# The second mixer's triangular inverse: diagonal blocks packed in DRAM, four partitions for each, and a transpose on TensorE

## The chip, the cores and the metric

The kernel runs as one program on 1 core of one Trainium2 chip. The metric is the device time of that core in microseconds (us), the median over repeated runs. TensorE (PE in the rows; PEld is its weight load) does the matmuls, VectorE is DVE, ScalarE is ACT, GpSimd is POOL, and SyncE is SP, which here only issues DMAs. A line such as L403 is line 403 of the kernel before; lines of the changed kernel are named as such.

## The reference, cut to what matters

Two transformer blocks of width 1024 run over one sequence of 256 tokens. The second block's token mixer holds two linear recurrences, each with 4 heads of width 128: a gated delta rule (the kernel's `gdn`) and HGRN2 (the kernel's `hgrn`). Their gated outputs are joined and projected (`w_out`), and a mixture of 64 experts follows. The gated delta rule needs a unit lower triangular system solved per head and chunk:

```python
    L = jnp.where(strict, jnp.einsum('bhncd,bhnsd->bhncs', kb, kc) * decay, 0.0)
    rhs = jnp.concatenate([vc * bc[..., None], kb * jnp.exp(gc)[..., None]], axis=-1)
    sol = lax.linalg.triangular_solve(L + jnp.eye(CHUNK, dtype=L.dtype), rhs,
                                      left_side=True, lower=True, unit_diagonal=True)
...
    oB = hgrn2_chunked(qB, kB, iB.reshape(B, T, HG_HEADS, HG_DV), logf).reshape(B, T, HG_V)
    oB = rms_norm_2(oB, hg_norm_w) * jax.nn.silu(gateB)
    o = jnp.concatenate([oA, oB], axis=-1).astype(h.dtype)
    return jnp.einsum('bte,ed->btd', o, w_out)
```

The kernel works on chunks of 128 tokens, which the algebra allows: 8 systems (4 heads, 2 chunks) of 128x128.

## The kernel before, in words

**Weights.** Projection weights come from DRAM in units of 128x1024 fp32 (512 KB). SP's one queue loads a unit into `raw` (L274); ACT rounds it to `whi` (L324), and DVE, or POOL for a list of units, subtracts to get the remainder `wlo` (L325). Each product is then three matmuls per 128x128 weight tile: `whi` with the high part, `whi` with the low part, `wlo` with the high part (L330 to L332 in `linear`, L352, L357 and L358 in `pair`).

**The second mixer.** `second_block` keeps six generators: `k` is `proj_gdn`, `f` is `proj_hgrn`, `q` is `proj_qv`, `h` is `hgrn`, `d` is `gdn`, `g` is `proj_gates2`. A string of letters, `MIXER`, says in which order they are stepped, and so in which order the work is recorded; a scheduler then fixes one order of instructions for each engine when the program is built, from its own estimates of durations. On the chip each engine runs its list in that order and waits where an operand is missing. `proj_gates2` makes the output gates from four pairs of 128x256 products, 48 matmuls a pair (L1304 to L1315); these, and the short convolutions of the projections (L1145, three taps per tile on DVE), are the work that stands beside the inverse.

**The inverse.** `proj_gdn` ends with `inverse(L, 8, self.N, "ax")` (L1239). L holds 8 matrices of 128x128, tokens on partitions. Each is cut into a 4x4 grid of 32x32 blocks. `inverse` writes L to DRAM (`dl`, L421) and reads the 32 diagonal blocks back with one block per partition (`inst`, L424). `base_inverse` then inverts all 32 at once by a forward elimination of 31 steps, two DVE instructions a step (the product at L403 into `kt`, the subtraction at L404), each over 32 partitions and (31-j)(j+1) elements. ACT writes the transposes (L405), both forms go to DRAM (`da`, L435), and seven reads put them where the products want them: four into N (L439), three into Mc (L442). Then TensorE fills the blocks off the diagonal by products of 32x32 and 64x64 blocks (L413, copies between at L454 to L477). The last write of N is the copy at L477.

**After it.** `gdn` for two chunks of 128 tokens uses N; the copy of its last product from PSUM is at L1373. `hgrn` takes its two chunks one after the other; each goes through seven levels (differences L1435 and L1436 and a product L1438 on DVE, exp on ACT at L306, a product on POOL at L1439, four matmuls L1441, a masked copy L1447 on DVE) and a diagonal (L1445, and L1447 with the mask `masks`). The state between chunks is copied at L1467, the output at L1476. `gated` (L1388, L1389) multiplies by the gates, and `mix_half` runs the output projection (L1404). The first mixer of the kernel calls `inverse` too, with 16 systems and an `extra` argument (L724).

## Time and profile before

| | |
|---|---|
| median of 3 runs | 1160.67 us (1160.2 to 1164.21) |
| profiled execution | 1161.43 us, its span 1159.6 us |
| busy in the span | PE 1078.0 us (93%), DVE 678.1 (58%), ACT 437.1 (38%), POOL 240.3 (21%) |
| mean granted TensorE clock | 0.975 of full speed |

The span is the stretch between the first and the last recorded instruction; the profiled execution's own time is 1.83 us more. The share of busy time is a mean over stages with different limits: the recursion of the second inverse, its products and both recurrences of the mixer lie between about 600 and 705 us of the span, and what limits that stretch is read there.

### The profile page before, as it was taken

The numbers are of one execution on the slowest core, as the hardware profiler recorded it, in microseconds if no ns is written. First come the engines' busy times: TensorE is split into PE (matmuls) and PEld (weight loads), VectorE is DVE, ScalarE is ACT, GpSimd is POOL, SyncE is SP. The second block draws the span as 40 slices with busy tenths as digits, with TensorE's granted clock in tenths as the row PEclk, the third lists the DMA queues.
The fourth block names the chain that finished last, engine by engine and source line by source line (L and its number), as shares of the span: only waits on it lengthen the run. The fifth ranks groups of instructions, "written<-read, shape, count | busy, mean of one in ns | idle before, by whom it ended". The sixth has DMA issues, their size and how long they took to land.

```text
span 1159.6 us, 20386 instructions
## 1 busy us (share of the span) xinstructions
PE 1078.0 (93%) x8050; PEld 824.7 (71%) x8050; DVE 678.1 (58%) x1211; ACT 437.1 (38%) x707; POOL 240.3 (21%) x245
## 2 busy tenths in 40 slices
PE   4989899999999999988979999999999999999995
PEld 4889787788989999987968889874444455444441
DVE  5598633356687888878799988432333333333333
ACT  5744433365454444335855645311111111111112
POOL 1251102023322001486461131320000000000000
PEclk9899979999999999999999999899999999999998
DMA  4445521025578998864434503969999999999993
GB/s 172 146 138 183 167 72 38 1 76 175 171 243 287 326 332 323 285 243 151 148 117 142 179 31 135 420 230 385 419 406 416 419 419 420 388 420 419 419 419 146
DMA packets 67496, 290.70 MB, mean 251 GB/s; under 512 B 15984, under 2 KB 17136, under 8 KB 46912
## 3 DMA queue, kind: packets, MB, share of 16 engines
q1 hardware_dynamic: 66528, 287.93, 66.3%
q8 instruction: 66, 1.08, 0.4%
q10 hardware_dynamic: 864, 1.38, 0.4%
q14 instruction: 38, 0.31, 0.1%
HBM read 285.77 MB, written 3.51 MB: 249 GB/s over the span
## 4 chain that ended last, share of the span: by engine, by line
PE 47%; DMA 17%; DVE 8%; ACT 4%; issue 4%; POOL 3%; SPq 0%; POOLq 0%; DVEq 0%; ACTq 0%
DMA er<-in_E_dram 12%; PE bank L1896 8%; PE p_b L357 4%; PE p_b L358 4%; PE p_b L352 4%; PE bank L1924 4%; PE acc L1793 3%; PE bank L1856 3%; DMA xa<-in_E_dram 3%; PE p_b L797 2%; POOL wlo L325 2%; ACT k L306 2%; PE p_b L332 2%; PE p_b L331 2%; PE p_b L330 2%
## 5 line engine op out<-in xcount | busy, mean ns | idle before, releaser
L324 ACT ACTIVATE whi<-raw 128x1024 fp32r<-128x1024 f32 x168 | 175.4, 1056 | 101.1 <-PE p_b L331 35.3
L325 DVE TENSOR_TENSOR wlo<-raw,whi 128x1024 fp32r<-128x1024 f32 x138 | 179.8, 1310 | 52.3 <-ACT whi L324 47.9
L358 PE MATMUL p_b<-k,wlo 128*128 128x256 f32 x608 | 173.6, 286 | 4.3 <-DVE wlo L325 2.4
L357 PE MATMUL p_b<-k,whi 128*128 128x256 f32 x608 | 173.9, 286 | 2.3 <-DVE k L325 2.3
L352 PE MATMUL p_b<-k,whi 128*128 128x256 f32 x608 | 173.5, 286 | 1.5 <-ACT whi L324 0.7
L332 PE MATMUL p_b<-k,wlo 128*128 128x256 f32 (+2 forms) x496 | 143.3, 294 | 14.5 <-DVE wlo L325 12.7
L330 PE MATMUL p_b<-k,whi 128*128 128x256 f32 (+2 forms) x496 | 145.5, 297 | 7.5 <-ACT k L324 4.1
L331 PE MATMUL p_b<-k,whi 128*128 128x256 f32 (+2 forms) x432 | 125.8, 294 | 2.1 <-DVE k L1126 1.1
L358 PEld LDWEIGHTS p_b<-k,wlo 128*128 128x128 f32 x608 | 116.6, 192 | 7.2 <-DVE wlo L325 3.0
L325 POOL TENSOR_TENSOR wlo<-raw,whi 128x1024 fp32r<-128x1024 f32 x30 | 81.0, 2704 | 193.8 <-ACT whi L324 193.1
L357 PEld LDWEIGHTS p_b<-k,whi 128*128 128x128 f32 x608 | 116.4, 192 | 3.7 <-DVE k L325 2.7
L352 PEld LDWEIGHTS p_b<-k,whi 128*128 128x128 f32 x608 | 116.3, 192 | 3.1 <-issue 0.9
L332 PEld LDWEIGHTS p_b<-k,wlo 128*128 128x128 f32 (+1 forms) x496 | 95.8, 195 | 17.3 <-DVE wlo L325 14.8
L330 PEld LDWEIGHTS p_b<-k,whi 128*128 128x128 f32 (+1 forms) x496 | 95.8, 195 | 13.3 <-ACT k L324 5.1
L1896 PE MATMUL bank<-er,x 128*32 128x512 f32 (+2 forms) x464 | 90.2, 595 | 3.3 <-DMA er<-in_E_dram 3.2
L1924 PE MATMUL bank<-er,k 128*32 128x512 f32 (+2 forms) x488 | 89.4, 595 | 2.6 <-DMA er<-in_E_dram 1.4
L1896 PE MATMUL bank<-er,h 128*32 128x512 f32 (+2 forms) x488 | 87.5, 595 | 0.0
L331 PEld LDWEIGHTS p_b<-k,whi 128*128 128x128 f32 (+1 forms) x432 | 84.5, 196 | 2.9 <-DVE k L1126 1.3
L1098 DVE SCALAR_TENSOR_TENSOR wada<-wada,crow 128x1024 f32<-128x1024 f32 x48 | 70.8, 1476 | 25.6 <-DMA wada<-in_W_ada_dram 25.3
L1844 POOL TENSOR_TENSOR k<-k,masks 128x128 f32<-128x128 f32 (+3 forms) x44 | 17.5, 430 | 316.0 <-DVE y L325 309.6
L1901 ACT ACTIVATE k<-bank 128x256 f32<-128x256 f32 x24 | 9.2, 385 | 194.6 <-PE bank L1896 194.6
L1902 DVE SCALAR_TENSOR_TENSOR k<-k,gs,bank 128x256 f32<-128x256 f32 x24 | 11.5, 480 | 100.1 <-ACT k L1901 100.1
(478 smaller groups left out, 2037.0 us busy)
## 6 DMA issues: line engine op xcount, KB each, us to landing
er<-in_E_dram SPq DMA_DIRECT2D x132, 1024.0 KB, 17.9
raw<-in_W_dram SPq DMA_DIRECT2D x168, 512.0 KB, 4.1
wada<-in_W_ada_dram SPq DMA_DIRECT2D x48, 512.0 KB, 5.7
xa<-in_E_dram SPq DMA_DIRECT2D x24, 1024.0 KB, 12.6
xa<-in_Sh_dram SPq DMA_DIRECT2D x2, 1024.0 KB, 8.3
k<-in_xT_dram SPq DMA_DIRECT2D x4, 272.0 KB, 5.0
dl<-x SPq DMA_DIRECT2D x1, 1024.0 KB
x<-in_xT_dram SPq DMA_DIRECT2D x1, 1024.0 KB
```

Of the source, the lines that this page charges most:

```text
L324: ins = self.nc.scalar.activation(hi, src, AF.Copy)
L325: (engine or self.nc.vector).tensor_tensor(lo, src, hi.bitcast(F32), op=OP.subtract)
L330: mm(out, w[0], x[0], start=start, stop=False)
L331: mm(out, w[0], x[1], start=False, stop=False)
L332: mm(out, w[1], x[0], start=False, stop=stop)
L352: a = mm(p[:, i], w[0], v[0], start=(n == 0), stop=False, **kw)
L357: mm(p[:, i], w[0], v[1], start=False, stop=False, **kw)
L358: mm(p[:, i], w[1], v[0], start=False, stop=last, **kw)
L1098: nc.vector.scalar_tensor_tensor(w, w, 1.0, c, op0=OP.mult, op1=OP.mult, accum_out=self.mod[:, o:o + 1])
L1793: self.nc.tensor.matmul(self.acc[t], w, x, start=t not in self.started, stop=False, skip_group_check=True)
L1896: mm(ph[t], X[:, k, i * 128 + t.start:i * 128 + t.stop], u[:, kk * 512:kk * 512 + 512], start=(k == 0), stop=(k == KD - 1), skip_group_che ...
L1924: nc.tensor.matmul(py[t], q.H[:, k, t], u[:, k * 1024 + c * 512:k * 1024 + c * 512 + 512], start=(k == 0), stop=(k == 1), skip_group_check ...
```

## The change

The inverse without `extra` (the second mixer's) goes through a new `by_columns`; with `extra` (the first mixer's) it goes through `by_blocks`, which holds the lines that were there. In `by_columns` the diagonal blocks alone are written to DRAM, one after the other (four writes of 32-KB pieces, 128 KB in all), and that 128 KB is read four times as a whole, to partitions 0 to 31, 32 to 63, 64 to 95 and 96 to 127. So every block stands on four partitions, and partition group c solves for columns c, c+4, c+8 and so on: 31 steps of two instructions as before, over 128 partitions and (31-j)(j//4+1) elements. ACT writes the transposes (128x256 elements), one write takes them to DRAM, and four reads put them into N. The blocks for Mc, which were read from DRAM, come from 8 transposes of N on TensorE (L389 by way of `tr`) and 6 copies on ACT (L444 of the changed kernel).

```diff
+    def by_columns(self, L, N, Mc, work, tag):
...
+        inst, M, MT = b(work[:, 1], 32), b(work[:, 2, :256], 8), b(work[:, 3, :256], 32)
+        u, flat = work[:, 2, 256:512], work[:, 2, :256]
+        nc.gpsimd.memset(flat, 0.0)
+        for c in range(4):
+            nc.gpsimd.memset(flat[32 * c:32 * c + 32, 8 * c::33], 1.0)
+        dl = self.dram.tile([4 * ns, 32, 32], F32, name=f"dl{ns}")
+        for k in range(4):
+            q = slice(32 * k, 32 * k + 32)
+            nc.sync.dma_start(dl[ns * k:ns * k + ns].rearrange("s t c -> t s c"), L[q, :, q])
+        for c in range(4):
+            nc.sync.dma_start(inst[32 * c:32 * c + 32], dl)
+        for j in range(31):
+            r, c = 31 - j, j // 4 + 1
+            v = u[:, :r * c].rearrange("p (a b) -> p a b", b=c)
+            nc.vector.tensor_tensor(v, inst[:, j + 1:, j:j + 1].to_broadcast([128, r, c]), M[:, j:j + 1, :c].to_broadcast([128, r, c]), op=OP.mult)
+            nc.vector.tensor_tensor(M[:, j + 1:, :c], M[:, j + 1:, :c], v, op=OP.subtract)
+        nc.scalar.activation(MT, M.rearrange("p a b -> p b a"), AF.Copy)
+        da = self.dram.tile([8, 128, 32], F32, name=f"da{ns}")
+        nc.sync.dma_start(da.rearrange("i p t -> p i t"), MT)
+        back = da.rearrange("i (c k s) t -> (i c) k s t", c=4, k=4)
+        for k in range(4):
+            q = slice(32 * k, 32 * k + 32)
+            nc.sync.dma_start(N[q, :, q], back[:, k])
+        yield
+        for h in (0, 4):
+            pt = b(self.psum(tag), 128)
+            for s in range(4):
+                self.tr(pt[:, s], N[:, h + s])
+            for k in range(3):
+                q = slice(32 * k, 32 * k + 32)
+                o = 32 * (k % 2)
+                nc.scalar.activation(Mc[q, h:h + 4, o:o + 32], pt[q, :, q], AF.Copy)
...
+        if not extra:
+            yield from self.by_columns(L, N, Mc, work, tag)
+        else:
+            yield from self.by_blocks(L, ns, N, Mc, work, extra)
```

The scheduler places the work after the recursion elsewhere. On TensorE, at the first product of the inverse, the order of before reads as follows; `p_b_7307` is the PSUM tile of the fourth and last pair of `proj_gates2`, and `p_b_6592` that of the inverse's first product.

```order
L357 MATMUL p_b_7307<-k_5673,whi 128x256
L358 MATMUL p_b_7307<-k_5672,wlo 128x256
L413 MATMUL p_b_6592<-k_6437,k_6075 32x32 x8
L352 MATMUL p_b_7307<-k_5672,whi 128x256
L357 MATMUL p_b_7307<-k_5673,whi 128x256
L358 MATMUL p_b_7307<-k_5672,wlo 128x256
```

In the order of the changed kernel (L413 is L481 there) the inverse's first product stands in the second pair, `p_b_7138`, and the transposes that feed Mc follow.

```order
L358 MATMUL p_b_7138<-k_5672,wlo 128x256
L352 MATMUL p_b_7138<-k_5672,whi 128x256
L481 MATMUL p_b_6609<-k_6437,k_6075 32x32 x8
L357 MATMUL p_b_7138<-k_5673,whi 128x256
L358 MATMUL p_b_7138<-k_5672,wlo 128x256
L1485 MATMUL p_b_7233<-h_7234 128x128 x4
L389 MATMUL p_b_6593<-masks,k_6437 128x128 x4
L389 MATMUL p_b_6601<-masks,k_6437 128x128 x4
L1485 MATMUL p_b_7245<-h_7246 128x128 x3
```

Before, 30 of the 48 matmuls of the fourth pair stand ahead of the inverse's first product; now 46 of 48 of the second pair do, and 83 matmuls of the third and fourth pairs come behind the inverse's last product, 79 of them ahead of `gdn`'s last (L1416 of the changed kernel).

On DVE, around `gdn`'s last copy, the order of before has the copy (L1373) among the levels of `hgrn`'s second chunk, whose tiles are the `h` from 7422 up; rows of the last four levels stand around it.

```order
L1447 COPY_PREDICATED h_7422<-offT,p_b_7454 128x512
L1435 TENSOR_TENSOR h_7503<-h_7424 128x128x2
L1436 TENSOR_TENSOR h_7503<-h_7424 128x128x2
L1438 TENSOR_TENSOR h_7503<-h_7503,h_7426 128x128x2
L1373 COPY k_6931<-p_b_7206 128x4x128
L1447 COPY_PREDICATED h_7422<-offT,p_b_7466 128x512
L1435 TENSOR_TENSOR h_7515<-h_7424 128x256
L1447 COPY_PREDICATED h_7422<-offT,p_b_7490 128x512
```

In the changed kernel that copy is L1417, the levels are L1479, L1480, L1482 and L1491, and the second chunk's tiles are the `h` from 7439 up.

```order
L1417 COPY k_6948<-p_b_7223 128x4x128
L1491 COPY_PREDICATED h_7060<-offT,p_b_7391 128x512
L1500 TENSOR_TENSOR h_7416<-h_7062 128x512
L1358 SCALAR_TENSOR_TENSOR k_6990<-p_b_7324,cols,ge 128x256 x2
L1502 TENSOR_TENSOR h_7416<-h_7416,h_7064 128x512
L1491 COPY_PREDICATED h_7060<-masks,p_b_7403 128x512
L1511 COPY h_7059<-p_b_7427 128x512
L1520 COPY k_7058<-p_b_7433 128x4x128
L1479 TENSOR_TENSOR h_7448<-h_7441 128x4x64
L1480 TENSOR_TENSOR h_7448<-h_7441 128x4x64
L1479 TENSOR_TENSOR h_7460<-h_7441 128x8x32
```

Before, `gdn`'s last copy comes after 18 of the second chunk's 21 differences and products; now the first chunk's last level, its diagonal and its state and output copies (`h_7058`, `h_7059`, `h_7060` and L1520) come behind `gdn`'s last copy, and the second chunk's first instruction is the ninth row.

## Rows read from the trace of the kernel before

**Rows 1.** Windows: stretch, length, busy us of PE, PEld, DVE, ACT, POOL; clock, DMA.

```profile
600.00:660.00 60.00, 50.01 (x396) 48.48 (x397) 58.62 (x118) 33.73 (x44) 12.97 (x7) 0.97 0.40 130
660.00:700.00 40.00, 37.78 (x353) 33.09 (x352) 32.82 (x58) 18.71 (x32) 13.08 (x14) 1.00 0.20 63
```

**Rows 2.** PE's timeline, 605 to 650: start, duration, instruction, wait and releaser.

```profile
607.33 0.39 PE L332 MATMUL p_b<-k,wlo 128*128 128x256 f32 x1 [4.71 <-DVE wlo L325]
...
649.17 0.39 PE L358 MATMUL p_b<-k,wlo 128*128 128x256 f32 x1 [1.61 <-DVE wlo L325]
```

**Rows 3.** DVE's timeline, the recursion of the second inverse from its first to last instruction.

```profile
600.53 0.72 DVE L403 TENSOR_TENSOR kt<-gate 32x31 f32<-32x31 f32 x1
601.28 0.20 DVE L404 TENSOR_TENSOR gate<-gate,kt 32x31 f32<-32x31 f32 x1
...
602.85 2.31 DVE L404 TENSOR_TENSOR gate<-gate,kt 32x112 f32<-32x112 f32 x1
...
627.58 0.46 DVE L1145 SCALAR_TENSOR_TENSOR k<-p_b,cols,k 128x253 f32<-128x253 f32 x1
627.98 0.40 DVE L404 TENSOR_TENSOR gate<-gate,kt 32x252 f32<-32x252 f32 x1
...
652.21 0.17 DVE L404 TENSOR_TENSOR gate<-gate,kt 32x31 f32<-32x31 f32 x1
```

**Rows 4.** POOL's timeline, the first of three splits in that stretch.

```profile
602.67 2.36 POOL L325 TENSOR_TENSOR wlo<-raw,whi 128x1024 fp32r<-128x1024 f32 x1 [1.47 <-ACT whi L324]
```

**Rows 5.** DVE's timeline behind the recursion: the inverse's last copy, gdn, hgrn's second chunk.

```profile
673.93 0.67 DVE L477 TENSOR_SCALAR k<-p_b 64x512 f32<-64x512 f32 x1
...
679.76 0.68 DVE L1343 TENSOR_TENSOR k<-p_b,k 128x512 f32<-128x512 f32 x1
680.36 0.42 DVE L1435 TENSOR_TENSOR h<-h 128x256 f32<-128x256 f32 x1
680.69 0.68 DVE L1348 TENSOR_TENSOR k<-p_b,k 128x512 f32<-128x512 f32 x1
...
683.25 0.95 DVE L1436 TENSOR_TENSOR h<-h 128x256 f32<-128x256 f32 x1
...
695.31 0.69 DVE L1373 COPY k<-p_b 128x512 f32<-128x512 f32 x1
```

**Rows 6.** ACT's timeline: the transposing copy of the recursion's result.

```profile
652.88 2.02 ACT L405 ACTIVATE gate<-gate 32x1024 f32<-32x1024 f32 x1
```

**Rows 7.** SP's timeline: the writes of that result and the reads behind them.

```profile
652.41 2.84 SPq L435 DMA_DIRECT2D da<-gate  x2
...
656.92 0.81 SPq L439 DMA_DIRECT2D k<-da  x2
```

**Rows 8.** The tile dl, both inverses, writes and reads together: its landing times.

```profile
DMA to landing us min/median/max: 2.6/4.9/5.2
```

**Rows 9.** The tile da, both inverses: its landing times.

```profile
DMA to landing us min/median/max: 1.8/3.1/3.7
```

**Rows 10.** PE's timeline: the pace of full matmuls, inverse products, transposes, the output projection's first.

```profile
612.04 0.28 PE L330 MATMUL p_b<-k,whi 128*128 128x256 f32 x1
...
615.95 0.28 PE L330 MATMUL p_b<-k,whi 128*128 128x256 f32 x1
...
662.30 0.69 PE L413 MATMUL p_b<-k,k 32*32 32x32 f32 x16
...
668.78 0.65 PE L389 MATMUL p_b<-masks,k 128*128 128x128 f32 x4
669.37 1.14 PE L413 MATMUL p_b<-k,k 64*64 64x64 f32 x16
...
703.26 0.60 PE L1404 MATMUL p_b<-yh,whi 128*128 128x256 f32 x3
```

**Rows 11.** Windows behind PE's first wait, and behind the mixer.

```profile
608.00:610.00 2.00, 2.00 (x12) 2.00 (x11) 1.90 (x5) 0.41 (x1) 0.00 (x0) 0.50 0.83 233
770.00:774.00 4.00, 3.86 (x12) 1.78 (x11) 2.05 (x6) 0.48 (x1) 1.63 (x4) 1.00 0.01 4
```

More of the change, by code (lines that the diff above doesn't have):

```diff
@@ L405, in base_inverse @@
         nc.scalar.activation(MT[:P], M.rearrange("p a b -> p b a"), AF.Copy)
-    def inverse(self, L, ns, N, tag, extra=None):
+    def by_columns(self, L, N, Mc, work, tag):
         nc = self.nc
-        mm = lambda out, l, r: nc.tensor.matmul(out, l, r, start=True, stop=True)
-        ne = 4 * ns + (8 if extra else 0)
-        nc.gpsimd.memset(N, 0.0)
-        work = self.alloc("gate", [4, 1024])
-        Mc = work[:, 0, :ns * 64].rearrange("p (a b) -> p a b", b=64)
-        nc.gpsimd.memset(Mc, 0.0)
+        ns = 8
+        b = lambda x, n: x.rearrange("p (a b) -> p a b", b=n)
+        inst, M, MT = b(work[:, 1], 32), b(work[:, 2, :256], 8), b(work[:, 3, :256], 32)
[30 more added lines that the diff above has]
+                nc.scalar.activation(Mc[q, h:h + 4, o:o + 32], pt[q, :, q], AF.Copy)
@@ L419, in inverse, with by_blocks @@
+    def by_blocks(self, L, ns, N, Mc, work, extra):
+        nc = self.nc
+        ne = 4 * ns + 8
         inst, A0, A1 = (work[:, i].rearrange("p (a b) -> p a b", b=32) for i in (1, 2, 3))
@@ L424, in inverse @@
             nc.sync.dma_start(inst[k * ns:(k + 1) * ns], dl[q, :, q].rearrange("t s c -> s t c"))
-        if extra:
-            dm = self.dram.tile([128, 2, 32], F32, name="dm")
-            nc.sync.dma_start(dm, extra[0])
-            for g in range(2):
-                o = 4 * ns + 4 * g
-                nc.sync.dma_start(inst[o:o + 4], dm[:, g].rearrange("(i t) c -> i t c", i=4))
+        dm = self.dram.tile([128, 2, 32], F32, name="dm")
+        nc.sync.dma_start(dm, extra[0])
+        for g in range(2):
+            o = 4 * ns + 4 * g
+            nc.sync.dma_start(inst[o:o + 4], dm[:, g].rearrange("(i t) c -> i t c", i=4))
         A = A0, A1
@@ L442, in inverse @@
                 nc.sync.dma_start(Mc[q, :, o:o + 32], da[0, s].rearrange("s t c -> t s c"))
-            if extra:
-                nc.sync.dma_start(extra[1][q, :, q], da[1, 4 * ns:].rearrange("(g i) t c -> i t g c", g=2)[k])
+            nc.sync.dma_start(extra[1][q, :, q], da[1, 4 * ns:].rearrange("(g i) t c -> i t g c", g=2)[k])
         yield
+    def inverse(self, L, ns, N, tag, extra=None):
+        nc = self.nc
+        mm = lambda out, l, r: nc.tensor.matmul(out, l, r, start=True, stop=True)
+        nc.gpsimd.memset(N, 0.0)
+        work = self.alloc("gate", [4, 1024])
+        Mc = work[:, 0, :ns * 64].rearrange("p (a b) -> p a b", b=64)
+        nc.gpsimd.memset(Mc, 0.0)
+        if not extra:
+            yield from self.by_columns(L, N, Mc, work, tag)
+        else:
+            yield from self.by_blocks(L, ns, N, Mc, work, extra)
         X = work[:, 1, :ns * 64].rearrange("p (a b) -> p a b", b=64)
```

## The prediction

> **What bounds the kernel now.** The share of busy time says TensorE, but it is a mean, so I went to the stretch of the change: first the windows, then PE's waits in them, then the lists of DVE, ACT and SP beside those waits. From 600 to 660 DVE is busy 58.62 of 60 us and PE 50.01 [rows 1]: DVE sets the pace there. PE's gaps end on a weight's low part that stands behind DVE's list, 4.71 us at 607.33 and 1.61 at 649.17 [rows 2]; with two smaller ones between they make some 8.8. What fills DVE is short convolutions, splits of weights, and the recursion of the second inverse, from 600.53 to 652.38 [rows 3]. From 660 to 700 it is the reverse: PE 37.78 of 40, DVE 32.82 [rows 1]. There the inverse's products start at 662.30 [rows 10], N's last copy ends at 674.60, gdn's last copy at 696.00 [rows 5], and the output projection begins at 703.26 [rows 10]. The last third is a stream of expert weights, but it can't swallow a shift of that point: from 770 to 774 the DMA engines are 0.01 busy while PE is 3.86 of 4 busy [rows 11]. The prefetch is full and waits for PE, so what the mixer's end gains or loses passes to the kernel's end.
>
> **The change, part by part.** *DVE.* Two instructions a step over (31-j)(j+1) elements come to 10,912 per partition in 31 steps; with (31-j)(j//4+1) it is 3,120. A 512-wide row takes 0.60 us to the next start, a 256-wide one 0.33 [rows 5], so an element is 1.05 ns and an instruction 0.06 to 0.07 more. The saving is 7,792 x 1.05 = 8.2 us of a DVE that is full. That the 62 instructions run on 128 partitions in place of 32 I price at nothing: the wide rows there have 128 already.
>
> Where does the recursion end? The order still starts it behind the same hgrn row, so at 600.53. Ahead of its end stand 9 weight splits at 1.14 us (1024 elements, 10.3), 24 convolution taps at 0.40 from 627.58 to 627.98 (9.6) [rows 3], one wide product (1.1); its own elements 3.3, 31 instructions with another between at 0.07 (2.2), 31 behind their own partner at the 0.20 of a small one [rows 3] (6.2). POOL's splits hold DVE: the one at 602.67 [rows 4] stretched a 112-element row to 2.31 [rows 3], 2.1 too long; three of them, 6.3. With one wait of 0.8, 39.8 us: the end is at **640.3**, 12 us earlier.
>
> *Copy and DMA.* ACT's transposing copy was 2.02 us for 1024 elements [rows 6]; a quarter is 0.5. The write is issued at 640.9. It has 1,024 pieces of 128 bytes into DRAM, which no row of before shows. From below: da's transfers land in 3.1 at the median [rows 9]; from above 5.2, the slowest of dl [rows 8]. I take 4.5, near the upper end, since the rows of dl that are slow are those with 128-byte pieces and with a weight load ahead of them in the queue, as here. The old pair of writes held SP 2.84 us, and reads went out 0.40 apart [rows 7]; four reads and 3.1 put N at about 648.8 for the second and 650 for the last. On the write side dl now goes out in small pieces too, some 2 us later at worst. The last read of it lay a good 4 us ahead of the recursion's start before, which waits for DVE's list, not for it: nothing. Three weight loads behind it move by as much, with raw buffers in hand: nothing, or 1 us if they are missed.
>
> *PE.* The inverse's first product now stands behind 46 of 48 matmuls of the second gate pair. Before, PE was at that matmul ten paces after 649.17 [rows 2]: at 650.4, a pace being 0.118 (33 from 612.04 to 615.95, rows 10). With DVE lighter I close 3 us of its waits but not the 4.71, which is POOL's doing: 647.3. So PE **waits about 1.5 us** for N at a place where it had filler before; queued behind are the rest of the pair and hgrn's last levels of the first chunk. From its first product to the last copy of N took 12.3 us, of which 4.9 was filler and about 1.1 a DVE that was held. Filler is now 15 gate matmuls (1.8), eight hgrn products (1.2) and waits (0.5); the eight transposes cost 1.2, since four take 0.59 to the next start [rows 10]; their ACT copies replace three reads. N is complete at **659.6**, 15 us earlier.
>
> *gdn.* From N to gdn's last copy took 21.4 us, with hgrn's second chunk as its filler (about 6.5 on PE). Now 79 to 83 gate matmuls are the filler, 9.4 to 9.8, and closed gaps give back about 1: 23.7, so the last copy ends at **683.3** (1.5 either way), 12.7 earlier.
>
> *The tail* is where it is lost. Before, hgrn's second chunk began on DVE at 680.36 [rows 5], in the shade of gdn, and only 7.3 us lay between gdn's last copy and the projection. Now the first chunk's last level, diagonal, state and output come behind gdn's last copy: six 512-wide rows and two 256-wide, 4.4 us, and a chain through PE's transposes, ACT's copy, and PE's products, some 3.0. The second chunk starts at 690.75, 10.4 later. Alone on DVE it takes seven levels of three 256-wide and one 512-wide row (1.6 each, 11.3), a diagonal 0.6, two rows of gdn's norm 1.2, gates and the last product 1.6, and holds by POOL's products, as in the 0.95 of 683.25 [rows 5], 2.0: 16.7. The projection starts at 707.45 against 703.26 [rows 10]: **4.2 us later**. POOL's smaller fills lie where POOL is free (13 of 60 us busy, rows 1).
>
> The profiled execution took 1161.43, the median is 0.76 less. 1161.43 + 4.2 - 0.76 = **1164.9 us**.
>
> Two rules bear on the parts that no row shows. The trace of before has no write of 128-byte pieces. The Trainium skill, page "DMA: Bandwidth & Descriptors", section "Specifications", wants 512 bytes or more in a transfer for the line's rate, since smaller ones are read, modified and written. No run here shows it yet; by it the write would end at or beyond my upper end, which is the third rival's condition. And PE's clock: after the 4.71 us wait the granted clock stood at 0.50 from 608 to 610 [rows 11], the lower of its two levels (1.2 of 2.4 GHz), with PE busy all the time. The Trainium skill, page "TensorE: Matmul & The Clock Gate", section "Part 1: The HAM clock gate", says that an array that has been little used is clocked at half; the trace agrees, with that 0.50. A thin tail, such as I forecast, is a place for it.
>
> **The rivals.** *The saving arrives.* DVE is the bound from 600 to 660, and 8.2 less transposes at 1.2 would give 1160.7 - 7.0 = **1153.7**. This needs gdn's last copy at 672, or a tail that overlaps; the static order of DVE speaks against it, since the second chunk's first row stands behind that copy. *No change.* The new wait of 1.5 at the first product does not arise (the write at the lower end, 3.1), the rest of PE's waits up to there close (1.1), and the products wait less (1.2): gdn's last copy is at 679.5, the projection at 703.6, the time **1161.1**. For it: PE's list holds the same work plus 1.2. *Slower yet.* The small pieces land at 6.5 (2 us more, straight onto PE, since N is what it waits for), and PE, with some 8 idle of 24 us in the tail, runs there at the 0.50 of 608 to 610 [rows 11]; of eight groups of four products, 0.5 each, about half lie bare in the chain, so 2 us more: 1164.9 + 4 = **1169**. It decides once N comes later than about 651. *The change doesn't do what it says.* If short rows over 128 partitions cost what chained ones cost, or the pieces for four partitions come late, the recursion ends at 644 rather than 640, N with it, and less is gained to pay for the tail: 1164.9 + 4 = **1168.9**.
>
> **How the numbers follow.** What can be told from no change is about 0.5%, so 1154.9 to 1166.5. The forecast, 1162 to 1167.5, has 0.50, a quarter of it past 1166.5; no change 0.17; the saving arrives 0.11; slower yet 0.15; not what it says 0.07. So faster 0.11; slower 0.125 + 0.15 + 0.07, less a little of the last that ends below the line, 0.32; same 0.57. The range leaves out the fast case and the far end of the slow one: 1158.5 to 1170.
>
> **What would show it.** Right: the recursion's last row near 640; the da write landing in 3 to 5 us; a PE wait on DMA of 1 to 3 us at L481; gdn's last copy (L1417) near 683; the second chunk's first L1479 near 691, and the projection's first matmul near 707, with DVE nearly full between. Wrong: a recursion that ends past 644; N landing ahead of PE; a clock of 0.5 in the tail; or a second chunk that takes 14 us rather than 16.7, or 20, since nothing in before shows it running alone. The tail's 7.45 and 16.7 are the least sure terms; they decide the sign.

## The result and the profile after

The changed kernel takes 1179.42 us (median of 4 runs, 1174.56 to 1182.09) against 1161.74 for the kernel before on the same chips; the ratio is 1.0136, with a 95% interval from 1.0096 to 1.0176. It is slower by some 16 us by the ratio and 18 by the medians, where 1164.9 and a range up to 1170 were forecast. Its profiled execution took 1182.09 us, span 1180.4.

The windows of the changed kernel that answer to [rows 1], and one long window of each kernel: from the last matmul that makes L to the last matmul of the output projection. First the kernel before, then the changed one; columns as in [rows 1].

```profile
580.57:734.78 154.21, 138.30 (x1151) 130.06 (x1149) 133.28 (x251) 79.95 (x127) 45.81 (x40) 0.99 0.41 140
```

```profile
584.90:753.23 168.33, 149.25 (x1159) 139.83 (x1157) 124.95 (x251) 81.15 (x133) 49.95 (x40) 0.92 0.37 126
600.00:660.00 60.00, 51.38 (x404) 49.99 (x402) 53.38 (x117) 32.68 (x49) 17.73 (x13) 0.89 0.47 151
660.00:700.00 40.00, 37.63 (x306) 33.36 (x304) 18.78 (x29) 15.81 (x25) 7.90 (x7) 0.87 0.19 61
604.00:618.00 14.00, 10.57 (x55) 10.36 (x54) 12.27 (x31) 4.86 (x6) 4.70 (x5) 0.63 0.46 148
662.00:672.00 10.00, 10.00 (x48) 7.25 (x49) 2.25 (x4) 2.81 (x5) 2.35 (x1) 0.51 0.11 34
706.00:710.00 4.00, 3.92 (x21) 3.94 (x21) 2.86 (x6) 1.89 (x3) 0.67 (x2) 0.58 0.00 0
```

The long window grew by 14.1 us. Ahead of it the changed kernel's execution was already 4.3 late (584.90 against 580.57), before any changed instruction; this start lies anywhere from 577 to 590 in the traces below, on either kernel, so it is not put down to the change. Behind the window both take nearly as long (424.8 and 427.2 us to the span's end): what the mixer loses does reach the end.

DVE's busy time falls from 133.28 to 124.95 us, by 8.3: the saving is there, as large as worked out (8.2). From 600 to 660 DVE is busy 53.38 us, against 58.62 in [rows 1]. From 660 to 700 it is busy 18.78, against 32.82, since hgrn's second chunk, which stood there before, now comes later. What grows is PE's time. Idle is the window less its busy time: 15.9 before, 19.1 after. What half clock adds is about the window times one less the mean clock: 0.01 x 154.2 = 1.5 before, 0.08 x 168.3 = 13.5 after (to 0.8 or so, as the clock column has two digits). What is left is 136.8 and 135.8, the same work at full clock. So by this account 12 of the 14 us are what half clock adds to PE's time, in four places: behind its first two waits (604 to 618, clock 0.63), behind its third (638.20 to 641.6, where a 128x256 matmul takes 0.41 us in place of 0.28), in the second half of the inverse (662 to 672, 0.51) and in the lone second chunk (706 to 710, 0.58). The account says how PE spent the time, not that each of these microseconds lengthened the kernel.

DVE's timeline of the changed kernel, from the recursion's first instruction (L427) to hgrn's second chunk (L1479); it answers to [rows 3] and [rows 5].

```profile
601.52 2.13 DVE L427 TENSOR_TENSOR gate<-gate 128x31 f32<-128x31 f32 x1 [0.80 <-DMA gate<-dl]
603.68 0.69 DVE L428 TENSOR_TENSOR gate<-gate 128x31 f32<-128x31 f32 x1
...
606.43 0.22 DVE L428 TENSOR_TENSOR gate<-gate 128x29 f32<-128x29 f32 x1
...
608.17 2.33 DVE L427 TENSOR_TENSOR gate<-gate 128x50 f32<-128x50 f32 x1
...
646.42 0.16 DVE L428 TENSOR_TENSOR gate<-gate 128x8 f32<-128x8 f32 x1
...
668.42 0.68 DVE L521 TENSOR_SCALAR k<-p_b 64x512 f32<-64x512 f32 x1 [5.52 <-PE p_b L481]
...
693.59 0.69 DVE L1417 COPY k<-p_b 128x512 f32<-128x512 f32 x1 [6.57 <-PE p_b L1416]
...
702.12 0.42 DVE L1479 TENSOR_TENSOR h<-h 128x256 f32<-128x256 f32 x1
```

The recursion ends at 646.6 (652.4 before), N is complete at 669.1 (674.6), gdn's last copy ends at 694.3 (696.0), and only then does hgrn's second chunk start, at 702.12 (680.36 before).

Counted from the end of L, which takes the late start out, the stages read as follows.

| us from the last matmul of L (580.57 and 584.90) | before | changed |
|---|---|---|
| the recursion ends | 71.8 | 61.7 |
| N's last copy ends | 94.0 | 84.2 |
| gdn's last copy ends | 115.4 | 109.4 |
| the projection starts | 122.7 | 137.2 |

So the shorter recursion does arrive: 10 us at its end and 6 at gdn's last copy. The whole loss stands between that copy and the projection, which lie 27.8 us apart and lay 7.3 apart before. Half clock ahead of the copy eats part of the gain; it is behind the copy that the changed kernel falls behind the old one.

PE's timeline of the changed kernel: its waits over 1.4 us, and some products of the inverse; it answers to [rows 2] and [rows 10].

```profile
603.65 0.39 PE L332 MATMUL p_b<-k,wlo 128*128 128x256 f32 x1 [2.39 <-POOL wlo L325]
611.94 0.58 PE L332 MATMUL p_b<-k,wlo 128*128 128x256 f32 x1 [3.43 <-DVE wlo L325]
638.20 0.41 PE L352 MATMUL p_b<-k,whi 128*128 128x256 f32 x1 [2.14 <-DVE gate L428]
...
654.70 0.69 PE L481 MATMUL p_b<-k,k 32*32 32x32 f32 x16
...
662.95 1.97 PE L481 MATMUL p_b<-k,k 64*64 64x64 f32 x16
...
697.18 1.13 PE L1489 MATMUL p_b<-h,h 128*128 128x128 f32 x8 [1.83 <-DVE k L1358]
...
704.85 2.80 PE L1485 MATMUL p_b<-h 128*128 128x128 f32 x16 [1.88 <-POOL h L1483]
...
715.04 2.11 PE L1485 MATMUL p_b<-h 128*128 128x128 f32 x16 [1.47 <-DVE h L1482]
...
722.12 0.39 PE L1448 MATMUL p_b<-yh,whi 128*128 128x256 f32 x1
```

The three waits up to 640 sum to 8.0 us, hardly less than the 8.8 of before. A group of 64x64 products takes 1.97 us where it took 1.14 [rows 10]; a group of 32x32 products takes 0.69 in both, so that only the second half of the inverse is slowed. The projection starts at 722.12 against 703.26.

The DMA view of the changed kernel, 640 to 660: KB each and us from issue to landing; it answers to [rows 7 to 9].

```profile
da<-gate SPq DMA_DIRECT2D x1, 128.0 KB, 4.5
k<-da SPq DMA_DIRECT2D x4, 32.0 KB, 2.0
```

The write of 1,024 small pieces lands in 4.5 us, the value taken from between 3.1 and 5.2. The two 128-KB writes of before, in 4-KB pieces, landed in 2.8 (median). The Trainium skill, page "DMA: Bandwidth & Descriptors", section "Specifications", counts pieces under 512 bytes as below the line's rate; the trace agrees in direction, with 4.5 against 2.8. The 6.5 us of the third rival it was not.

### The profile page after: what moved, and what is told of

The parts are those of the page before. It is cut to its first block, busy times and chain, and to the rows that moved or that the text cites. A ratio compares the mean times of both kernels' runs of the same rounds, so it can differ in the third digit from the quotient of the medians.

```text
span 1180.4 us, 20420 instructions
## 1 busy us (share of the span) xinstructions
PE 1093.7 (93%) x8058; PEld 835.1 (71%) x8058; DVE 674.2 (57%) x1211; ACT 438.4 (37%) x713; POOL 242.4 (21%) x248
## 4 chain that ended last, share of the span: by engine, by line
PE 45%; DMA 18%; DVE 10%; ACT 4%; issue 3%; POOL 2%; SPq 0%; ACTq 0%; POOLq 0%; DVEq 0%
DMA er<-in_E_dram 11%; PE bank L1940 9%; PE bank L1968 4%; DMA wada<-in_W_ada_dram 4%; PE p_b L357 3%; PE p_b L358 3%; PE p_b L352 3%; PE acc L1837 3%; PE bank L1900 3%; DVE wlo L325 2%; PE p_b L841 2%; DVE wada L1142 2%; ACT k L306 2%; DMA xa<-in_E_dram 2%; PE p_b L332 2%
## 5 line engine op out<-in xcount | busy, mean ns | idle before, releaser
L358 PE MATMUL p_b<-k,wlo 128*128 128x256 f32 x608 | 176.1, 290 | 6.8 <-DVE wlo L325 5.0
L352 PE MATMUL p_b<-k,whi 128*128 128x256 f32 x608 | 175.3, 289 | 3.6 <-DVE gate L428 2.1
L357 PE MATMUL p_b<-k,whi 128*128 128x256 f32 x608 | 176.4, 290 | 2.3 <-DVE k L325 2.3
L330 PE MATMUL p_b<-k,whi 128*128 128x256 f32 (+2 forms) x496 | 147.0, 300 | 6.3 <-ACT k L324 4.1
L331 PE MATMUL p_b<-k,whi 128*128 128x256 f32 (+2 forms) x432 | 127.1, 296 | 2.1 <-DVE k L1170 1.1
L352 PEld LDWEIGHTS p_b<-k,whi 128*128 128x128 f32 x608 | 117.7, 194 | 5.6 <-issue 3.2
L357 PEld LDWEIGHTS p_b<-k,whi 128*128 128x128 f32 x608 | 117.9, 194 | 4.3 <-DVE k L325 2.7
L330 PEld LDWEIGHTS p_b<-k,whi 128*128 128x128 f32 (+1 forms) x496 | 97.2, 198 | 11.9 <-ACT k L324 5.1
L331 PEld LDWEIGHTS p_b<-k,whi 128*128 128x128 f32 (+1 forms) x432 | 86.0, 200 | 2.9 <-DVE k L1170 1.3
L1142 DVE SCALAR_TENSOR_TENSOR wada<-wada,crow 128x1024 f32<-128x1024 f32 x48 | 75.1, 1566 | 21.4 <-DMA wada<-in_W_ada_dram 21.3
L1946 DVE SCALAR_TENSOR_TENSOR k<-k,gs,bank 128x256 f32<-128x256 f32 x24 | 11.5, 481 | 101.8 <-ACT k L1945 101.8
```

The lines of the kernel that those rows point to most:

```text
L330: mm(out, w[0], x[0], start=start, stop=False)
L331: mm(out, w[0], x[1], start=False, stop=False)
L352: a = mm(p[:, i], w[0], v[0], start=(n == 0), stop=False, **kw)
L357: mm(p[:, i], w[0], v[1], start=False, stop=False, **kw)
L358: mm(p[:, i], w[1], v[0], start=False, stop=last, **kw)
L1142: nc.vector.scalar_tensor_tensor(w, w, 1.0, c, op0=OP.mult, op1=OP.mult, accum_out=self.mod[:, o:o + 1])
```

## Experiments

All of them but the three with fills (e4, e7, e12) compute what the reference asks for with the same instructions in another order, or on another engine. The account in the last three columns is that of the long window above, by the same three sums, from each run's profiled execution; the ratio is to the kernel before on the same chip. One execution can lie well off the median (e17's took 1153.3 us where its median is 1163.2), so differences of a few us between accounts are not to be read as differences between kernels.

| run | median us | ratio, 95% interval | idle | half clock | rest |
|---|---|---|---|---|---|
| before | 1161.7 | | 15.9 | 1.5 | 136.8 |
| changed | 1179.4 | 1.0136, 1.0096 to 1.0176 | 19.1 | 13.5 | 135.8 |
| e1 before, serial tail | 1173.3 | 1.0094, 1.0059 to 1.0130 | 22.5 | 1.6 | 139.6 |
| e2 changed, hgrn recorded first | 1171.6 | 1.0082, 1.0053 to 1.0111 | 16.7 | 8.1 | 136.7 |
| e3 changed, products spread | 1177.0 | 1.0139, 1.0094 to 1.0184 | 21.6 | 8.3 | 135.7 |
| e4 changed, products filled | 1180.2 | 1.0184, 1.0128 to 1.0240 | 20.5 | 5.1 | 143.6 |
| e5 changed, late inverse | 1180.8 | 1.0166, 1.0120 to 1.0212 | 22.1 | 6.6 | 135.6 |
| e6 changed, early inverse | 1172.7 | 1.0076, 1.0045 to 1.0107 | 21.4 | 6.5 | 134.6 |
| e7 changed, light fill | 1173.8 | 1.0112, 1.0056 to 1.0168 | 20.2 | 4.9 | 139.5 |
| e8 before, late inverse | 1184.2 | 1.0201, 1.0152 to 1.0249 | 23.4 | 10.2 | 136.1 |
| e9 changed, gdn first | 1171.3 | 1.0067, 1.0037 to 1.0097 | 17.2 | 6.4 | 135.4 |
| e10 before, gdn first | 1175.9 | 1.0113, 1.0070 to 1.0155 | 21.5 | 6.6 | 136.2 |
| e11 changed, pairs before inverse | 1167.4 | 1.0028, 0.9994 to 1.0063 | 15.2 | 4.7 | 136.0 |
| e12 changed, hgrn first, light fill | 1170.6 | 1.0046, 1.0014 to 1.0078 | 16.4 | 3.2 | 138.9 |
| e13 changed, two splits to DVE | 1171.3 | 1.0060, 1.0021 to 1.0099 | 16.8 | 6.4 | 135.8 |
| e14 e11, two splits to DVE | 1168.1 | 1.0047, 1.0017 to 1.0077 | 13.3 | 6.3 | 137.1 |
| e15 changed, four splits to DVE | 1165.8 | 1.0010, 0.9977 to 1.0042 | 13.2 | 3.0 | 136.0 |
| e16 before, two splits to DVE | 1169.7 | 1.0052, 1.0025 to 1.0078 | 16.5 | 6.4 | 136.1 |
| e17 e11, four splits to DVE | 1163.2 | 0.9993, 0.9972 to 1.0013 | 11.5 | 3.0 | 135.6 |
| e18 before, four splits to DVE | 1159.4 | 0.9964, 0.9943 to 0.9985 | 11.6 | 1.5 | 136.5 |

**Two theories first.** A: the loss is hgrn's second chunk alone behind gdn. B: it is PE's half clock over the inverse's products, and the later recursion.

**e1, the kernel before with a serial tail.** On the kernel before:

```diff
-            nc.vector.tensor_copy(o[:, :, tok], po)
+            self.gdn_end = nc.vector.tensor_copy(o[:, :, tok], po)
...
+                    if b:
+                        self.order(a, self.gdn_end)
...
-MIXER = 'kkkffkfkkfkfffffffkfqkkqqqqqqqqddghhfdhhgdhhgghhhhhhdhhhghh'
+MIXER = 'kkkffkfkkfkfffffffkfqkkqqqqqqqqddghhfdhhgdhhgghhdhhhhhhhhhghh'
```

Here `a` is the first difference of a level (L1435).

> The kernel before, its recursion and inverse untouched, with one thing forced: hgrn's second chunk may not start on DVE ahead of gdn's last copy, as in the changed kernel. Theory A (the loss is hgrn's second chunk standing alone behind gdn): the first levels wait for gdn's copy near 690, then about 8 + 18 us as in the changed kernel's trace (694.3 to 702.1 to 722), so the projection starts 10 to 15 us later and the time is 1171 to 1177. Theory B (the loss is PE's half clock while the inverse's products run without full matmuls beside them, and the later recursion): those stay as they were here, so the tail costs 2 us or less, 1162 to 1164.

DVE's timeline of this run, the copy of gdn and the second chunk's first row, and its long window:

```profile
692.05 0.69 DVE L1373 COPY k<-p_b 128x512 f32<-128x512 f32 x1 [6.56 <-PE p_b L1372]
692.66 0.74 DVE L1435 TENSOR_TENSOR h<-h 128x256 f32<-128x256 f32 x1
```

```profile
579.85:743.56 163.71, 141.21 (x1151) 130.70 (x1149) 134.90 (x251) 80.25 (x127) 51.03 (x40) 0.99 0.39 134
```

Theory A's number: the place of one chunk costs 0.94% (about 11 us) without any change to the inverse, and the long window grows by 9.5, 6.6 of it PE's idle time. From the second chunk's first row to the projection's first matmul at 709.26 it takes 16.6 us, where the prediction had 16.7. The clock stays at 0.99, so a serial tail does not need half clock to be dear.

**e2, the changed kernel with hgrn recorded first.**

```diff
-MIXER = 'kkkffkfkkfkfffffffkfqkkqqqqqqqqddghhfdhhgdhhgghhhhhhdhhhghh'
+MIXER = 'kkkffkfkkfkfffffffkfqkkqqqqqqqqghhhhhhhhfddghhdgdhhgghhhdhhh'
```

> The changed kernel with another order of recording only: hgrn's first chunk ahead of gdn, two gate pairs later, so that all seven levels of hgrn's second chunk start on DVE ahead of gdn's last copy. Theory A: the loss of some 14 us of the tail goes, 1163 to 1168. Theory B: the inverse's products still run at half clock from about 662 to 672, N is complete where it was, and no more than 4 us is won: 1175 or more.

1.0082: some 6 us less than the changed kernel, between the two theories; the intervals overlap. Its windows over the products and behind them:

```profile
654.00:664.00 10.00, 10.00 (x61) 8.00 (x59) 2.18 (x5) 0.97 (x2) 0.52 (x1) 0.52 0.08 32
678.00:710.00 32.00, 30.19 (x231) 28.33 (x230) 26.34 (x48) 16.71 (x25) 11.91 (x10) 0.95 0.25 75
```

Idle time is back at 16.7, but the stretch of the products still runs at 0.52. Both theories seem to hold a part.

**e3, products spread.** The last of the two `k` steps of the inverse is recorded behind two gate pairs (`...fqkqqqqqqqqghhfhhghhgkddhhdhhghhhhhdhhhghh`).

> The changed kernel with another order of recording only: one gate pair ahead of the inverse's products and hgrn's first chunk too, so that the products stand among the third pair's matmuls and hgrn's second chunk among gdn. Theory A: 1161 to 1168, like the run with hgrn recorded first, whatever the clock does. Theory B: clock 1.00 over the products, 4 us less between first product and N's last copy than in the changed kernel (14.4), and most of the loss gone only here: 1165 or less, clearly below the run with hgrn recorded first.

Both expectations missed (1.0139). Only the 64x64 products went behind the third pair, the 32x32 ones stayed, and the stretch from first product to N's last copy grew from 14.4 to 18.5 us (649.41 to 667.94). The 64x64 products took 1.14 us a group again. A full clock alone buys nothing if the chain is pulled apart.

**e4 and e7, fills.** Behind each group of eight products of the second inverse:

```diff
-                mm(px[p][f, s], L[z, s, f], N[z, s, z])
+                last = mm(px[p][f, s], L[z, s, f], N[z, s, z])
+            if not extra:
+                self.keep_busy(1, 512, last)
```

(and so for the other four kinds of product; 128 in place of 512 in e7).

> The changed kernel with seven more 128x128 by 512 matmuls that nobody reads, one behind each group of eight products of the inverse (computation added, none left out). If the half clock there comes from an array that holds only 32x32 and 64x64 products, the clock from 662 to 672 is 1.00, the products' groups of eight take 0.35 us in place of 0.69, and the added 3.7 us of matmuls about eat what is won: time within 3 us of the changed kernel's 1179. If the clock falls for another reason it stays at 0.50 and the time rises by 5 us or more, 1184.

> The changed kernel with seven more matmuls that nobody reads, as in the run with filled products, but of 128 columns in place of 512 (1.9 us in place of 7.5). If these already hold the clock at 1.00 over the inverse's products, the stretch from first product to N's last copy falls from 14.4 to 11 or 12 and the time to 1175 to 1178; if 128 columns are too few, the clock falls to 0.50 as in the changed kernel and the time is 1179 to 1182.

The window over the products, in e4 and in e7:

```profile
650.00:664.00 14.00, 13.39 (x132) 8.70 (x132) 4.74 (x9) 5.66 (x14) 2.42 (x2) 1.00 0.22 72
```

```profile
650.00:664.00 14.00, 13.22 (x148) 10.93 (x149) 4.64 (x9) 6.27 (x14) 3.40 (x2) 1.00 0.20 68
```

With either fill the clock is 1.00 where it was 0.51. That the fill did it is not shown, for two runs below have no fill: e13, in the changed kernel's recorded order (PE's list differs a little), has its 64x64 products at full clock (first row), and e14, with the same sequence of PE's instructions over the inverse as e11, has them at half (second row) where e11 has them at full.

```profile
663.94 1.14 PE L481 MATMUL p_b<-k,k 64*64 64x64 f32 x16
```

```profile
661.05 1.97 PE L481 MATMUL p_b<-k,k 64*64 64x64 f32 x16
```

So what stands among the products does not settle the clock, and what does stays open. What it costs can be read from that pair: from the first product to N's last copy e14 takes 11.6 us, e11 8.1. In the changed kernel it is 14.4, in e13 12.9. The large fill costs what it wins (1.0184 against 1.0136, the rest column 143.6). The small one: 1173.8 against 1179.4 by the medians, 1.0112 against 1.0136 by the ratios, whose intervals overlap; and products to N's last copy take 15.1 us, not 11 or 12. That the clock over the products is worth 3 to 6 us of the kernel's time is likely, not shown. **e12** puts e7's fill on e2:

> The run with hgrn recorded first (1171.6) and the seven 128-column matmuls that nobody reads together. If the half clock over the products (654 to 665 there) and the lone second chunk are two separate losses, they add up: 3 to 6 us less than hgrn first, 1165 to 1169. If the fill won only because the second chunk was late, no gain: 1171 to 1174.

1.0046 against e2's 1.0082: 4 us by the ratios, half clock 3.2 in place of 8.1, again with intervals that overlap; the median of 1170.6 lies between the two expectations.

**Theory C, PE's account; theory D, the parts of the change cost time in any order.** The two runs with one recorded order, on either kernel:

```diff
-MIXER = 'kkkffkfkkfkfffffffkfqkkqqqqqqqqddghhfdhhgdhhgghhhhhhdhhhghh'
+MIXER = 'kkkffkfkkfkfffffffkfqqqqqqqqqghhfhhghhghhgkkddhhdhhhhhdhhhghh'
```

> The changed kernel, order of recording alone: all four gate pairs and hgrn's first chunk are recorded ahead of the inverse's products and of gdn, so that on TensorE the products come after three pairs and among the fourth, and hgrn's second chunk starts ahead of gdn's last copy. Theory C (what was lost is TensorE's time: from the making of L to the last matmul of the output projection it has 136 us of work at full clock in every order, and the rest is idle time plus what half clock adds, 15.9 + 1.7 before and 19.1 + 13.2 in the changed kernel): idle 13 to 16, half clock 1 to 3, 1158 to 1164. Theory D (the change's own parts, small pieces in DRAM, short rows on 128 partitions and transposes, cost time in any order): the 8 us of the run with hgrn recorded first stay, 1169 to 1173.

> The kernel before with the order of recording of the run with the late inverse, its recursion and DRAM traffic untouched: what that order is worth by itself. Theory C: on TensorE the order is nearly that of before, 1160 to 1166; the difference between this and the late inverse with the change is what the lighter DVE gives, 2 to 5 us in the change's favour. Theory D: the change with that order is 5 us or more slower than this.

> As the run with the late inverse, but the fourth gate pair is recorded behind gdn's first steps: the inverse's products come after three pairs with no pair among them, and the fourth pair fills behind. Theory C: half clock over the products, as in the changed kernel from 662 to 674, costs 4 to 6 us, hgrn's second chunk still stands beside gdn: 1164 to 1169. Theory D: 1169 to 1173, as with hgrn recorded first. If the clock over the products costs nothing, it equals the run with the late inverse.

Theory C missed in all three; e6's 1172.7 lies in theory D's range, e5 and e8 lie beyond both. The order itself is bad (1.0201 on the kernel before). gdn and hgrn's second chunk end together there (gdn's last copy ends at 706.57 in e5, the second chunk's last masked copy starts at 706.55), and PE then stands through gdn's norm and gating until 719.40, with waits of 1.87 and 3.04 us, where before hgrn's second chunk filled that time. In this order the changed kernel is the faster of the two, 1.0166 against 1.0201. In e6 (`...ghhfhhghhgkkddhhhdhhghhhhhdhhhghh`) the clock over the products was 1.00, against expectation; gdn's last copy comes 36.6 us behind N's (21.4 before), and the stand before the projection is there too (a wait of 3.06 us). So theory E: the loss is in how gdn, the second chunk and the gate pairs follow one another.

> The changed kernel, order of recording alone: the gate pairs and hgrn's first chunk ahead of the inverse's products as in the run with the late inverse, but all of gdn ahead of hgrn's second chunk, so that on DVE six of its seven levels start before gdn's last copy, as in the kernel before, and gdn ends first. Theory E (the loss lies in how gdn, hgrn's second chunk and the gate pairs follow one another, and what comes with it in half clock; the recursion by columns itself saves a little): gdn ends some 8 us ahead of the late inverse's run and the projection with it, 1160 to 1167. Theory D (the change's own parts cost time): 1170 or more.

> The kernel before with the order of recording of the run with gdn first; recursion and DRAM traffic untouched. It is the match for that run: Theory E: 1163 to 1170, and the changed kernel is 2 to 5 us faster in the same order, as with the late inverse (1180.8 against 1184.2). Theory D: the changed kernel is slower than this one by 3 us or more.

With all of gdn recorded first (`...ghhfhhghhghhgkkdddddhhhhhhhhhg`) the changed kernel comes to 1.0067 and the kernel before to 1.0113: both slower than theory E expected, and the changed one's 1171.3 within theory D's range; but the changed one is ahead by 4.6 us, against theory D, with overlapping intervals.

**e11, pairs before the inverse** (`...fqqqqqqqqqgghhfgghhkkddhhdhhdhhdhhhhhhhg`).

> The changed kernel, order of recording alone: all four gate pairs stand on TensorE ahead of the inverse's first product, gdn and hgrn take turns, four levels of the second chunk start ahead of gdn's last copy. Theory E: the pairs fill TensorE while DVE does the recursion, nothing waits for N, but the products run without full matmuls beside them (half clock, some 5 us): 1165 to 1172, a little slower than gdn first. Theory D: 1170 or more.

1.0028, not to be told from the kernel before, and with every part of the change in it: a loss of 8 us or more that the parts bring to any order, as theory D had it, falls. Whether this order would make the kernel before faster too was not run. PE's timeline of e11 over the inverse:

```profile
666.37 1.24 PE L481 MATMUL p_b<-k,k 32*32 32x32 f32 x32
667.54 0.71 PE L1485 MATMUL p_b<-h 128*128 128x128 f32 x4
668.18 1.50 PE L481 MATMUL p_b<-gate 32*32 32x32 f32 x48
669.61 0.94 PE L1485 MATMUL p_b<-h 128*128 128x128 f32 x6
670.48 1.14 PE L481 MATMUL p_b<-k,k 64*64 64x64 f32 x16
671.55 1.16 PE L1485 MATMUL p_b<-h 128*128 128x128 f32 x8
```

```profile
666.37:674.85 8.48, 8.48 (x134) 7.35 (x134) 4.76 (x10) 3.63 (x10) 0.84 (x1) 1.00 0.22 68
```

The chain of products takes 8.1 us to N's last copy (14.4 in the changed kernel), at clock 1.00 with hgrn's 128x128 matmuls between them. On DVE four levels of the second chunk start ahead of gdn's last copy, and from that copy to the projection it is 10.7 us.

**The recursion and POOL.** Units 143 and 145 (149 and 151 too, in the runs with four) are taken off the list of units that POOL splits:

```diff
-POOLU = (17, ... 121, 140, 143, 145, 149, 151, 158, 161)
+POOLU = (17, ... 121, 140, 149, 151, 158, 161)
```

> The changed kernel with two weight splits (units 143 and 145, at 601 and 608 in its trace) on DVE in place of POOL, nothing else. If the recursion ended 6 us later than worked out because POOL's work holds DVE (2.13, 2.33, 2.43 and 2.44 us for rows of 0.22), two of the holds go, 4 us, and two splits of 1.14 come: the recursion takes 42 us in place of 45, PE's waits of 2.39 and 3.43 for these units shrink and with them the half clock behind them; the time 1175 or a little less, since the lone second chunk remains. If PE sets the pace there at half clock, the recursion takes 45 as before and the time stays at 1179.

DVE's timeline of e13, the recursion's first and last row, and PE's wait beside it:

```profile
606.88 0.21 DVE L427 TENSOR_TENSOR gate<-gate 128x31 f32<-128x31 f32 x1
...
648.06 0.15 DVE L428 TENSOR_TENSOR gate<-gate 128x8 f32<-128x8 f32 x1
```

```profile
613.22 0.58 PE L332 MATMUL p_b<-k,wlo 128*128 128x256 f32 x1 [3.48 <-DVE wlo L325]
```

The recursion takes 41.3 us, near the 42 worked out for two holds fewer. Of the rows over 2 us two are left, 2.43 at 625.65 and 2.40 at 633.10, each beside one of the two splits left on POOL (from 624.78 and 633.01); e15, with none, has no such row. So the holds are POOL's. The Trainium skill, page "GPSIMD Engine Reference", section "1. Specifications", says that GpSimd shares its SBUF interfaces with VectorE, with contention for DVE instructions that have two SBUF inputs; the 2.33 us of 608.17 beside POOL's split agree. Of PE's two waits at these units one is gone and the other stays: the split that PE needs stands behind fourteen rows of the recursion on DVE, and the half clock behind it stays. The time fell further than expected, to 1.0060. The other five:

> The run with the pairs ahead of the inverse (1167.4, the best order so far), with the same two splits on DVE. With both causes off, the tail and the waits that end in half clock, the lighter DVE should show: 1159 to 1164, at or below the kernel before. If the holds by POOL are not what the waits come from, 1166 to 1169.

> The changed kernel with the four weight splits that POOL does beside the recursion (units 143, 145, 149 and 151) on DVE; the scheduler then also starts three levels of hgrn's second chunk ahead of gdn's last copy. No hold is left in the recursion but four splits of 1.14 come: 8.8 less 4.6, so it takes some 41 us; with three levels ahead, part of the tail is won too: 1167 to 1173. If neither counts, 1177 or more.

> The kernel before with the same two splits on DVE, as the match for the changed ones. Its DVE is full from 600 to 660, so that each split moved there costs 1.14 and saves a hold of 2.1: within 2 us of before, 1160 to 1164. If it falls to 1158 or less, a gain of the pairs-first run with the same move is not the change's.

> The changed kernel with the pairs ahead of the inverse and the four weight splits beside the recursion on DVE: the two best pieces together. If they add up (the order took 12 us off the changed kernel, the four splits 13), not all twice: 1158 to 1163. If both win the same stretch, the tail, it stays at 1165 to 1168.

> The kernel before with the same four splits on DVE, the match for the changed kernel with four splits (1165.8). Its DVE is full beside the recursion; with two splits it was 7 us slower. If a lighter DVE is what the change gives, this one pays for all four: 1168 to 1176, slower than the changed kernel with the same move. If the move is good by itself, 1160 or less.

e14 missed (1.0047, no better than e11): half clock rose to 6.3, since the clock over its 64x64 products was 0.50 this time. e16 missed too: the kernel before loses 0.5% by the same move. e15's time fell a little further than expected, to 1.0010, but not by a shorter recursion, which takes 43.3 us there in place of the 41 expected. It is the tail: with three levels of the second chunk ahead of gdn's last copy, that copy ends at 685.55 and the projection starts at 701.62, 16.1 us later, in place of 27.8. DVE's copy, PE's first matmul of the projection, and the long windows of e15, e17 and e18:

```profile
684.87 0.68 DVE L1417 COPY k<-p_b 128x512 f32<-128x512 f32 x1
```

```profile
701.62 0.62 PE L1448 MATMUL p_b<-yh,whi 128*128 128x256 f32 x3
```

```profile
580.59:732.77 152.18, 139.03 (x1158) 131.58 (x1157) 121.83 (x255) 81.53 (x133) 40.55 (x36) 0.98 0.42 143
```

```profile
576.99:727.06 150.07, 138.60 (x1159) 131.26 (x1157) 123.13 (x255) 81.18 (x133) 43.03 (x36) 0.98 0.42 142
```

```profile
578.38:727.93 149.55, 137.97 (x1150) 129.92 (x1149) 129.00 (x255) 80.81 (x127) 35.92 (x36) 0.99 0.42 143
```

e18 overturned its expectation: the kernel before with four splits more on DVE is the fastest of all, 0.9964 (0.9943 to 0.9985), although its DVE is the fuller one. The changed kernel with the same four splits is 5 us slower than it by the ratios, and with the pairs ahead it equals the kernel before (e17, 0.9993).

## Why the prediction was wrong

Point by point, by its own terms (forecast, then the changed kernel's trace):

- **DVE's saving**: 8.2 us; 8.3 by the busy time. Right.
- **The recursion's end**: 640.3; 646.6. The first step that failed, 6.3 us late: 1.0 by the start, 5.3 by the length (39.8; 45.1). Counted from L it is 2.0 (59.7; 61.7), since the recursion starts 16.6 us behind L here and started 20.0 behind it in the trace of before. The dl read was priced at nothing and held the start by 0.8 (0.5 in e4, 1.0 in e7). Four splits and a run of four products by POOL held DVE by some 10.2 us, where three splits and 6.3 were counted (the rows of 0.62 to 0.69 from 603.68 on, for 0.22 without POOL). The rest is PE: it waited 2.39 and 3.43 us, then ran at half clock to 618, and DVE waited in turn, 2.23 us at 619.18 for ACT's copy of PE's result. In e4 and e7, with the same order up to there, the recursion took 42.7 and 43.0 us against 45.1 here, so some 2 us are this execution's.
- **Copy, write, reads**: the write's landing 4.5, as taken; the reads 2.0 in place of 3.1; PE's new wait 0.3 us in place of 1.5. The wait that was to take the old one's place hardly exists.
- **"I close 3 us of PE's waits"**: 0.8 closed. The sums of waits are 8.8 and 8.0. One of the two waits of before that the prediction calls smaller is 1.72 us, at 632.12, and ends on POOL's split, not on DVE's list.
- **Products to N's last copy**: 10.8; 14.4. Mis-sized by 3.6: PE's clock stood in this term at nothing, and it was half from 662 on (64x64 groups 1.97 for 1.14).
- **gdn**: 23.7; 25.2. **Copy to second chunk**: 7.45; 7.8. **The second chunk alone**: 16.7; 20.0 to the projection, with waits of 1.88, 0.97 and 1.47 on POOL and DVE and clock 0.58 from 706 to 710; e1's, at full clock, took 16.6.

Together 6.3 - 0.4 + 3.6 + 1.5 + 0.4 + 3.3 = 14.7, the projection at 722.1 for 707.45. Less the 4.3 us of the late L it is 10.4: 6.7 up to gdn's last copy, where a gain of 12.7 us was forecast and 6.0 came, and 3.7 in the tail, where 24.15 was forecast and 27.8 came. Three of the prediction's own signs of being wrong came with it: a recursion past 644, a clock near 0.5 in the tail, a second chunk of 20 us.

The mechanism, a second chunk alone behind gdn, was right, and e1 shows that it is dear by itself: 0.94%, on a kernel that has nothing else of the change. What failed are terms of the sum: the gain ahead of gdn's last copy was put at twice its size (12.7 for 6.0), with PE's clock over the products at nothing and POOL's holds at 6.3 of 10.2 us, and the second chunk was short by 3.3. How much of the 6.7 each made is not shown. The clock stood in one rival alone, at 2 us in the tail. There it adds 1.7 (706 to 710); the other 11.8 of its 13.5 us lie where no term named it, behind PE's waits and in the second half of the inverse. The other half of that rival, a write that lands at 6.5, did not come (4.5). The rival with the saving arriving was wrong in the time, though 6.0 us did arrive at gdn's last copy. The one in which the change does not do what it says had its sign (past 644) but not its cause: rows of 50 to 76 elements on 128 partitions take 0.20 to 0.23 us without POOL, as taken.

The loss does not come with the parts of the change in every order: e11 has them all and lies at 1.0028, though its order was not tried on the kernel before. e15 and e17 have them too and lie at 1.0010 and 0.9993, but their move of splits also makes the kernel before faster (e18, 0.9964). What the recursion by columns is worth in the kernel's time stays open. It was compared on both kernels in five arrangements: 3.4 and 4.6 us for it (e5 and e8, e9 and e10), nearly level (e13 and e16, 1.0060 and 1.0052), 5 against it (e15 and e18), and 16 to 18 against it in the arrangement of the change itself. The intervals of the first four pairs overlap, and the scheduler makes each pair's engine orders a little different. How much of the changed kernel's 17 us falls to the tail and how much to PE's clock is bounded only: about 6 by e2, 11 by e1 for the first; about 3 to 6 by e7 and e12 for the second.

## What to carry to other kernels

A part made shorter in a kernel whose scheduler orders everything by its own estimates also moves what stands behind it: compare the orders first, and price the moved pieces, since here one chunk's place is worth 11 us (e1) and the saved work 8. Account for the bounding engine over the whole stretch (work at full clock, idle, what half clock adds); the first stayed between 134.6 and 137.1 us in 16 of the 17 kernels without fills (e1 has 139.6), and the other two told where to look. Then count each stage from one common event, since such an account does not tell which microsecond delays the end: here the gain of 6 us at gdn's last copy and the loss of 20 behind it can be seen only so.

## What the runs showed of the hardware

- The inverse's 64x64 products ran at a granted clock of 0.51 in the changed kernel (662 to 672, 1.97 us a group) and at full clock in e13 (1.14 us a group). One sequence of products, with hgrn's 128x128 matmuls among them, ran them at full clock in e11 and at half in e14, which cost 3.4 us to N's last copy. The Trainium skill, page "TensorE: Matmul & The Clock Gate", section "Part 1: The HAM clock gate (the "warmup" mystery)", ties the clock to how busy the engine has been; here PE's busy column shows 10.00 of 10.00 us at 0.51, so that column does not tell the clock.
- A DVE instruction of 8 elements on 128 partitions takes 0.16 us, of 76 elements 0.23, and another instruction behind it starts 0.08 to 0.14 us after it; beside POOL's products (L1483) rows of 29 to 31 elements take 0.62 to 0.69, and beside one of POOL's splits of 128x1024 a row of 50 to 70 elements takes 2.33 to 2.44.
- The order of the instructions, and the engine of four of them, move the kernel before from 1159.4 us (e18) to 1184.2 (e8) with the arithmetic unchanged.
